# Moving token tiles and weight tiles by 64 bytes within SBUF

## The chip, the cores and the metric

The kernel runs on one NeuronCore of a Trainium2 chip. Its time is the device time of one execution in microseconds. Before the change three timed runs lie between 2381.85 and 2384.83 us, with a median of 2383.91 us.

## The reference, cut to what matters

The reference is a two-layer trunk over 1024 latent tokens of width 1024 with 256 context tokens, all in float32. Nearly all of its arithmetic is in products of a token matrix with a weight matrix:

```python
proj = h @ w_in                                   # both mixers, in
out  = concat([fourier_mix(f_in), y]) @ w_out     # layer 0, out
out  = concat([sgu, pool_out]) @ w_out            # layer 1, out
jnp.square(jax.nn.relu(h @ w1)) @ w2              # each layer's MLP, 1024 -> 4096 -> 1024
```

Around these stand norms with adaLN modulation, a bidirectional SSD scan and a Fourier mix in layer 0, and a chunked spatial gate and a multi-scale pooling in layer 1.

## The kernel before, in words

**How a product is made.** Each float32 operand is split into two tiles of type fp32r, `hi` and `lo`: ScalarE casts `hi` (L489), VectorE subtracts to get `lo` (L490). `mm3` then issues three matmuls for every 128-deep slice, high by high, high by low, low by high. In each matmul one operand is stationary (a 128x128 slice that LDWEIGHTS loads into TensorE) and the other streams through as the moving operand, mostly 512 columns of 4 bytes, a row of 2,048 bytes in each partition. All of this is issued at one line, L478, so the tile names tell the matmuls apart: the profile writes `psg<-hhi,whi` for output, moving tile, stationary tile.

**Two arrangements.** In most products the weights stand still and tokens stream (`psg<-hhi,whi`, `psg<-rlo,whi`, `psg<-h,wlo` and so on): the input projections, both output projections and both MLPs. `Weights.get` and `gemm_tile` hand `mm3` the weight slices first. In two places it is the other way round, because the result is wanted with tokens on partitions: `gate` in `ssd_forward` (`psg<-whi,h`), and `v_gemm` and `v_seq` in `layer1_mixer` (`psg<-whi,hhi`). There a 128-token slice stands still and weights stream. `v_seq(0, 1)` is one such pass of 96 matmuls. After it the pooling group goes on with tokens streaming.

**Where tiles lie.** SBUF pools form two stacks. Pools opened without a side grow upward from the low addresses: `consts` first, from 8,320 to 11,140, then the token pools `h0`, `h1`, `hc` and later `actA`, `actB`, `actC`, the first at 11,168. Pools opened with `side="right"` grow downward from 229,344: among them `w`, the pool of 14 weight tiles of 4,096 bytes, which takes 172,000 to 229,344. Every token tile and every weight tile is a multiple of 512 bytes long, and so are the slices that matmuls take of them, apart from the last blocks of the kernel, which take 1,024-byte halves of token rows. So in the kernel before every moving token row starts at 416 modulo 512 (11,168 = 21 x 512 + 416) and every slice of a weight tile at 480 modulo 512 (172,000 = 335 x 512 + 480). In the two arrangements the same tiles change roles: a streaming weight row starts at 480, a standing token slice at 416. One exception streams tokens against a small projection tile, `wdt`, that lies elsewhere. Pools start at multiples of 32 bytes.

**What sets the order.** TensorE takes its matmuls in program order, with the MLPs interleaving seven products per step (`ORDER`, after a Strassen-like scheme, `PRODUCTS`). Weights come in on the SP queue, scratch stores go out on the POOL queue. VectorE and ScalarE make splits and sums ahead of TensorE.

**The lines that matter below.** `setup` opens the `consts` pool and allocates its first tiles; `run` opens `w`. L478 is `mm`, L489 and L490 are `split`. `startup` is the beginning of the program. The MLP's `FfnNorm` (L198 to L236) stands between each output projection and its MLP.

Of the kernel before, what the change touches and what calls it, by code (L numbers as in the profile page):

```python
# [9 lines left out]
F32 = mybir.dt.float32  # L10
# [6 lines left out]
P = 128  # L17
# [437 lines left out]
class Trunk:  # L455
# [78 lines left out]
    def setup(self):  # L534
        nc, a = self.nc, self.a
        self.cp = self.pool("consts")
        self.dp = self.pool("dram", space=DRAM)
        cp = self.cp
        cmat = cp.tile([P, 2 * P], F32, name="cmat")
        for n, m in ((0, 0), (1, 5)):  # L540
            nc.sync.dma_start(cmat[:, n * P:(n + 1) * P], a["cmat"][:, m * P:(m + 1) * P])
        self.ident, self.ones = cmat[:, :P], cmat[:, P:]
        self.eps = cp.tile([P, 1], F32, name="eps")
        nc.vector.memset(self.eps, EPS)
        self.nhalf = cp.tile([P, 1], F32, name="nhalf")
        nc.vector.memset(self.nhalf, -0.5)
        self.onecol = self.ones[:, 0:1]
        warm = cp.tile([P, 1], F32, name="warm")
        nc.scalar.activation(warm, self.eps, AF.Silu)
        self.cols = cp.tile([P, 2, P], F32, name="cols")  # L550
        self.silu = cp.tile([P, KT, 2], F32, name="silu")
        self.ada = cp.tile([P, 12, KT], F32, name="ada")
        self.adac = cp.tile([P, 2, KT], F32, name="adac")
        self.amul = cp.tile([P, 5, KT], F32, name="amul")
# [1389 lines left out]
```

## Time and profile before

| | before |
|---|---|
| timed runs, median (lowest to highest) | 2383.91 us (2381.85 to 2384.83) |
| the profiled execution's own time | 2386.13 us |
| its span, first to last instruction | 2384.3 us |
| TensorE matmul (PE) busy | 2333.1 us, 98% |
| weight load (PEld) busy | 1837.4 us, 77% |
| VectorE (DVE) busy | 1598.7 us, 67% |
| ScalarE (ACT) busy | 986.6 us, 41% |
| GpSimd (POOL) busy | 178.2 us, 7% |
| mean granted TensorE clock | 0.997 |

Busy shares say how much of the span an engine had an instruction in flight. Matmuls are pipelined: one that is listed with 399 ns overlaps the one behind it, so what a matmul costs is not its listed duration but the distance from its start to the next one's start. That distance is read from the timeline, or from a window with no idle time by dividing its length by the matmuls that start in it.

### The profile page before, as it was taken

To read this page: it belongs to the slowest core of one execution; us is meant where nothing else is said; L and a number is where in the kernel's file an instruction comes from. 1 tells how busy PE (TensorE), PEld (TensorE's weight loads), DVE (VectorE), ACT (ScalarE), POOL (GpSimd) and SP (SyncE) were. 2 spreads that over 40 slices of the span, in tenths; PEclk is the share of its full clock that TensorE was granted. 3 is DMA by queue.
4 is the path that set the end of the run, shared out by engine and by line. 5 is a ranking of instruction groups with operands and counts; after the bars stand their busy time and mean duration, and the time that the engine had idled before them with its cause. 6 is when DMAs were issued, how large, how long until landed. Compare 5 with 4: busy or idle time off the path is not lost. (4 is left out here: it accounts for less than half of the span.)

```text
span 2384.3 us, 27844 instructions
## 1 busy us (share of the span) xinstructions
PE 2333.1 (98%) x10445; PEld 1837.4 (77%) x10445; DVE 1598.7 (67%) x2100; ACT 986.6 (41%) x1385; POOL 178.2 (7%) x301
## 2 busy tenths in 40 slices
PE   7999999999999999999999999999989999999998
PEld 2787777777867888878888887888768888788887
DVE  4777777766378576777877638642496555887785
ACT  3656754443145443623443322121255444543241
POOL 0003002111001010100001000000000101000000
PEclk9999999999999999999999999999999999999999
DMA  8535567658415565873444125652133436754423
GB/s 301 169 125 166 160 217 244 197 183 289 129 58 185 181 219 193 282 250 98 174 171 133 58 71 181 220 208 89 62 117 132 168 126 227 256 186 168 135 82 111
DMA packets 305170, 400.52 MB, mean 168 GB/s; under 512 B 22064, under 2 KB 222380, under 8 KB 297612
## 3 DMA queue, kind: packets, MB, share of 16 engines
q1 hardware_dynamic: 257952, 297.75, 38.4%
q0 software_dynamic: 30656, 91.78, 10.6%
q10 hardware_dynamic: 16427, 9.22, 1.3%
q8 instruction: 82, 1.34, 0.2%
q14 instruction: 53, 0.43, 0.1%
HBM read 282.27 MB, written 116.39 MB: 167 GB/s over the span
## 5 line engine op out<-in xcount | busy, mean ns | idle before, releaser
L478 PE MATMUL psg<-hhi,whi 128*128 128x512 f32 x1088 | 433.4, 399 | 10.0 <-ACT hhi L489 5.7
L478 PE MATMUL psg<-hlo,whi 128*128 128x512 f32 x1088 | 432.2, 397 | 3.9 <-DVE hlo L490 3.9
L478 PE MATMUL psg<-hhi,wlo 128*128 128x512 f32 x1088 | 429.9, 396 | 0.0
L478 PE MATMUL psg<-rhi,whi 128*128 128x512 f32 (+1 forms) x920 | 361.4, 393 | 3.6 <-DVE lat L1545 3.6
L478 PE MATMUL psg<-rlo,whi 128*128 128x512 f32 (+1 forms) x920 | 360.5, 392 | 0.0
L478 PE MATMUL psg<-rhi,wlo 128*128 128x512 f32 (+1 forms) x920 | 360.2, 392 | 0.0
L478 PEld LDWEIGHTS psg<-hhi,whi 128*128 128x128 f32 x1088 | 204.6, 188 | 63.9 <-ACT hhi L489 8.0
L489 ACT CAST whi<-ww 128x1024 fp32r<-128x1024 f32 (+1 forms) x128 | 131.1, 1024 | 284.6 <-DVE wlo L490 233.3
L478 PEld LDWEIGHTS psg<-hlo,whi 128*128 128x128 f32 x1088 | 204.5, 188 | 55.9 <-DVE hlo L490 6.2
L478 PEld LDWEIGHTS psg<-hhi,wlo 128*128 128x128 f32 x1088 | 204.5, 188 | 50.2 <-issue 1.0
L490 DVE TENSOR_TENSOR wlo<-ww,whi 128x1024 fp32r<-128x1024 f32 (+1 forms) x128 | 152.0, 1187 | 106.6 <-PE psg L478 96.7
L1545 DVE SCALAR_TENSOR_TENSOR lat<-psg,ada,lat 128x512 f32<-128x512 f32 (+1 forms) x220 | 163.0, 742 | 81.6 <-PE psg L478 66.9
L478 PEld LDWEIGHTS psg<-rhi,whi 128*128 128x128 f32 x920 | 173.0, 188 | 45.5 <-issue 4.0
L478 PEld LDWEIGHTS psg<-rlo,whi 128*128 128x128 f32 x920 | 173.0, 188 | 40.3 <-issue 0.2
L478 PEld LDWEIGHTS psg<-rhi,wlo 128*128 128x128 f32 x920 | 173.0, 188 | 40.3
L478 PE MATMUL psg<-h,whi 128*128 128x512 f32 (+1 forms) x672 | 197.3, 375 | 4.3 <-DVE h L509 2.8
L489 ACT CAST whi<-ws 128x1024 fp32r<-128x1024 f32 (+1 forms) x96 | 97.8, 1021 | 182.1 <-PE psg L478 98.2
L478 PE MATMUL psg<-yhi,whi 128*128 128x512 f32 x384 | 154.1, 402 | 2.9 <-ACT nss L133 1.8
L478 PE MATMUL psg<-ylo,whi 128*128 128x512 f32 x384 | 152.4, 397 | 0.0
L478 PE MATMUL psg<-yhi,wlo 128*128 128x512 f32 x384 | 152.4, 397 | 0.0
L490 DVE TENSOR_TENSOR wlo<-ws,whi 128x1024 fp32r<-128x1024 f32 (+1 forms) x96 | 113.9, 1187 | 55.3 <-PE psg L478 49.4
L489 ACT CAST rhi<-rlo 128x1024 fp32r<-128x1024 f32 x116 | 115.9, 1047 | 75.6 <-PE psg L478 47.5
(296 smaller groups left out, 3578.4 us busy)
## 6 DMA issues: line engine op xcount, KB each, us to landing
rlo<-r_d SPq DMA_DIRECT2D x58, 1024.0 KB, 6.8
ww<-in_ffn_w_dram SPq DMA_DIRECT2D x190, 256.0 KB, 5.4
r_d<-rt POOLq DMA_DIRECT2D x64, 512.0 KB, 6.5
araw<-in_ada_w_dram SPq DMA_DIRECT2D x56, 512.0 KB, 4.8
r_d<-uc POOLq DMA_DIRECT2D x36, 512.0 KB, 2.9
lat<-lat_d SPq DMA_DIRECT2D x32, 512.0 KB, 10.6
ws<-in_ffn_w_dram SPq DMA_DIRECT2D x62, 256.0 KB, 3.4
wraw<-in_ev_w_in_dram SPq DMA_DIRECT2D x24, 512.0 KB, 7.5
```

Of the source, the lines that this page charges most:

```text
L478: self.nc.tensor.matmul(out, lhsT=lhsT, rhs=rhs, start=start, stop=stop, skip_group_check=onto)
L489: self.nc.scalar.copy(hi, x)
L490: self.nc.vector.tensor_tensor(lo, x, hi.bitcast(F32), ALU.subtract)
L1545: nc.vector.scalar_tensor_tensor(lt, ps, g(ct), lt, ALU.mult, ALU.add)
```

## The change: what it does

Two tiles of 16 float32 per partition (64 bytes) are allocated in `setup` and set to zero on GpSimd. Nothing reads them. One is the first tile of `consts`, so every pool of the low stack starts 64 bytes higher. The other is in a pool of its own that is opened first on the right, so every pool there starts 64 bytes lower. Token rows then start at 480 modulo 512 and weight slices at 416 modulo 512. The constants, the small tiles and all scratch tiles of both stacks move by the same 64 bytes. PSUM and the order of all other instructions stay.

```diff
@@ -536,6 +536,9 @@
         self.cp = self.pool("consts")
         self.dp = self.pool("dram", space=DRAM)
         cp = self.cp
+        self.place = [cp.tile([P, 16], F32, name="place"), self.pool("place", side="right").tile([P, 16], F32, name="wplace")]
+        for t in self.place:
+            nc.gpsimd.memset(t, 0.0)
         cmat = cp.tile([P, 2 * P], F32, name="cmat")
         for n, m in ((0, 0), (1, 5)):
             nc.sync.dma_start(cmat[:, n * P:(n + 1) * P], a["cmat"][:, m * P:(m + 1) * P])
```

## Rows read from the trace of the kernel before

**Rows 1.** The page: busy time, and the granted TensorE clock in forty slices.

```profile
PE 2333.1 (98%) x10445; PEld 1837.4 (77%) x10445; DVE 1598.7 (67%) x2100; ACT 986.6 (41%) x1385; POOL 178.2 (7%) x301
PEclk9999999999999999999999999999999999999999
```

**Rows 2.** Groups by line and form, PE: shape, count | busy us, mean ns | idle.

```profile
L478 PE MATMUL psg<-hhi,whi 128*128 128x512 f32 x1088 | 433.4, 399 | 10.0 <-ACT hhi L489 5.7 <-DVE uc L1585 2.2 <-ACT uc L1583 2.1
L478 PE MATMUL psg<-rhi,whi 128*128 128x512 f32 x888 | 352.0, 396 | 3.6 <-DVE lat L1545 3.6
L478 PE MATMUL psg<-h,whi 128*128 128x512 f32 x512 | 169.2, 405 | 4.3 <-DVE h L509 2.8 <-ACT h L508 1.0 <-ACT xr L118 0.4
L478 PE MATMUL psg<-yhi,whi 128*128 128x512 f32 x384 | 154.1, 402 | 2.9 <-ACT nss L133 1.8 <-ACT yhi L489 1.1
L478 PE MATMUL psg<-h,wlo 128*128 128x512 f32 x256 | 101.9, 399 | 0.0
L478 PE MATMUL psg<-whi,h 128*128 128x512 f32 x256 | 88.5, 417 | 0.0
L478 PE MATMUL psg<-whi,hhi 128*128 128x512 f32 x128 | 51.3, 401 | 0.0
L478 PE MATMUL psg<-h,whi 128*128 128x256 f32 x160 | 28.3, 279 | 0.0
```

**Rows 3.** Timeline, PE, weights streaming (`v_seq`): start us, us, engine, line, instruction.

```profile
1398.19 0.39 PE L478 MATMUL psg<-whi,hhi 128*128 128x512 f32 x1
...
1398.88 0.39 PE L478 MATMUL psg<-whi,hhi 128*128 128x512 f32 x1
...
1418.79 0.39 PE L478 MATMUL psg<-whi,hhi 128*128 128x512 f32 x1
```

**Rows 4.** Timeline, PE, tokens streaming, right behind that pass.

```profile
1420.18 0.39 PE L478 MATMUL psg<-hhi,whi 128*128 128x512 f32 x1
...
1441.18 0.39 PE L478 MATMUL psg<-hhi,whi 128*128 128x512 f32 x1
```

**Rows 5.** Windows of line L478 on PE: length, PE busy (matmuls in flight), clock, DMA.

```profile
1030.00:1318.00 288.00, 288.00 (x1236) 1.00 0.45 153
1780.00:2030.00 250.00, 250.00 (x1073) 1.00 0.51 174
2070.00:2350.00 280.00, 280.00 (x1202) 1.00 0.40 134
```

**Rows 6.** Timeline, PE, 256 columns of context tokens streaming, two stretches.

```profile
109.92 0.39 PE L478 MATMUL psg<-h,whi 128*128 128x256 f32 x2
...
114.68 0.39 PE L478 MATMUL psg<-h,whi 128*128 128x256 f32 x2
...
162.13 0.40 PE L478 MATMUL psg<-h,whi 128*128 128x256 f32 x2
...
164.25 0.40 PE L478 MATMUL psg<-h,whi 128*128 128x256 f32 x2
```

**Rows 7.** Groups by line and form, ACT and DVE, same operation on both sides.

```profile
L489 ACT CAST whi<-ww 128x1024 fp32r<-128x1024 f32 x120 | 126.1, 1051 | 269.5 <-DVE wlo L490 219.6 <-PE psg L478 39.7 <-DMA ww<-in_ffn_w_dram 10.1
L489 ACT CAST rhi<-rlo 128x1024 fp32r<-128x1024 f32 x116 | 115.9, 1047 | 75.6 <-PE psg L478 47.5 <-DMA rlo<-r_d 28.1
L490 DVE TENSOR_TENSOR wlo<-ww,whi 128x1024 fp32r<-128x1024 f32 x120 | 146.4, 1220 | 99.8 <-PE psg L478 89.9 <-ACT whi L489 9.5
L490 DVE TENSOR_TENSOR rlo<-rlo,rhi 128x1024 fp32r<-128x1024 f32 x116 | 138.9, 1218 | 6.6 <-ACT rhi L489 6.0
```

**Rows 8.** Windows, all engines: length, PE, PEld, DVE, ACT, POOL busy, clock, DMA.

```profile
0.00:110.00 110.00, 95.39 (x381) 53.80 (x382) 59.71 (x125) 49.76 (x99) 3.28 (x7) 1.00 0.74 244
688.00:730.00 42.00, 36.17 (x140) 26.40 (x139) 40.14 (x54) 21.41 (x26) 2.61 (x2) 0.92 0.19 61
1732.00:1773.00 41.00, 33.01 (x131) 23.69 (x131) 40.07 (x54) 20.56 (x26) 2.53 (x2) 1.00 0.14 43
2036.00:2063.00 27.00, 25.23 (x108) 19.68 (x107) 19.22 (x20) 16.26 (x18) 3.74 (x7) 1.00 0.93 327
```

**Rows 9.** Timeline, POOL, start of the program.

```profile
0.33 0.10 POOL L1932 MEMSET const-uint8-127<- 128x1 uint8 x1
```

**Rows 10.** Waits of PE: who waited for whom, us in total, times, longest.

```profile
PE psg L478 <- ACT hhi L489: 5.7, 4, 2.3
PE psm L486 <- DMA crow<-in_c_ctx_dram: 5.5, 1, 5.5
```

## The prediction

> **What bounds the kernel now.** [...] So 51 us at most are lost to PE standing idle, and the list of its waits shows them scattered: the two largest sources are 5.7 and 5.5 us [rows 10]. The bound is therefore the rate at which PE takes matmuls, and the next question is what one matmul costs. The listed 396 to 405 ns [rows 2] are latencies that overlap, so I went to the timeline for the distance from start to start.
>
> With weights streaming, one triple of matmuls starts at 1398.19 and the next at 1398.88 us; thirty triples later it is 1418.79 [rows 3]. That is 20.60 us for 90 matmuls, 228.9 ns each. Right behind it, with tokens streaming, 21.00 us pass between 1420.18 and 1441.18 [rows 4], again thirty triples: 233.3 ns each. The two stretches lie in one stage, have the same columns, the same clock and no waits.
>
> The difference is not an accident of this place. The windows of the MLPs are pure token streaming: 280.00 us with 1202 matmuls in flight, of which about two were already running at the left edge, so 1200 starts and 233.3 ns; the other two give 288.00/1234 = 233.4 and 250.00/1071 = 233.4 [rows 5]. Going through the timeline stretch by stretch, leaving out the first matmuls behind a break, I find 58 undisturbed stretches of token streaming, all at 233.3 ([rows 4] is one, the windows of [rows 5] hold the longest), and 20 of weight streaming in the gate and in `v_seq`/`v_gemm`, at 228.8 to 229.8 ([rows 3] is the last of them). No stretch of one kind has the rate of the other.
>
> What differs between the kinds? Streaming rows start at 416 modulo 512 and standing slices at 480 in the first kind; in the second it is 480 and 416. The change makes the first kind's addresses those of the second, and the reverse. Which of the two operands, or their distance, carries the 4.4 ns need not be known: the exchange swaps all three together. This is the step on which everything rests, and it is an inference from two kinds of products that differ in more than the address (which operand is the weight, and which half of SBUF it lies in).
>
> **The change part by part.**
>
> Token streaming, 512 columns. From the groups [rows 2]: 1088 with `hhi,whi` and as many each with `hlo,whi` and `hhi,wlo`, 3264; 888 three times for the `r` tiles, 2664; 512 `h,whi`; 384 three times for the `y` tiles, 1152; 256 `h,wlo`. Together 7848. Each goes from 233.3 to 228.9: 7848 x 4.4 = 34.5 us less.
>
> Weight streaming, 512 columns. 256 `whi,h`, and 128 each of `whi,hhi` and three like it, 768 [rows 2]. Each goes the other way: 768 x 4.4 = 3.4 us more.
>
> Token streaming, 256 columns. 160 `h,whi` [rows 2] and some 190 in smaller groups. These run at two rates with the same addresses: 14 triples from 109.92 to 114.68 us, 113.3 ns each, and six from 162.13 to 164.25, 117.8 each [rows 6]. So here the rate is set by something that the start of a stretch decides. All of them at one rate or the other is worth at most 350 x 4.4/2 = 0.8 us either way; I take zero.
>
> Small true-float32 matmuls, transposes, and columns by one: before, no row compares the same form at both offsets. As bounds I take the same 4.4 ns for each of the remaining 1,480 matmuls or so (10445 less 7848, 768 and 350) either way: 6.5 us, and choose zero, since a stretch of them mixes many offsets already.
>
> VectorE, ScalarE and transfers. The same cast of 1024 columns takes 1051 ns on weight tiles at 480 and 1047 on token tiles at 416; the same subtraction 1220 and 1218 [rows 7]. So the exchange is worth nothing there: 4 ns over the 116 to 120 instructions of a group is 0.5 us, on engines with a third or more of the span free. Transfers into both kinds of tiles keep their length, and move by whole 64 bytes; PE's largest wait for one is 5.5 us at the very start [rows 10], which no SBUF place of a later tile touches. Cost zero.
>
> The two memsets. The nearest row is a memset of 0.10 us on POOL in its first microsecond [rows 9]; POOL has 3.28 us of work in the first 110 us [rows 8]. Both sides: 0 to 0.2 us, hidden by PE's wait for the first transfer of 5.5 us. I take zero.
>
> What of the gain does not arrive. A faster PE gains only where the next thing it needs is there. In 688 to 730 and 1732 to 1773 us VectorE is busy for 40.14 of 42 and 40.07 of 41 us [rows 8] with the split that stands between output projection and MLP; PE's 271 matmuls there gain nothing: 1.2 us. In the first 110 us PE stands for 15 us behind loads and splits [rows 8], with some 190 token matmuls between: 0.8 us. Before each MLP's down half the first set goes out to DRAM and back (2036 to 2063, DMA at 0.93 [rows 8], and the like in layer 0): 108 matmuls each, 1.0 us together. VectorE is next to be late in each, and it is not sped up. Sum 3.0 us; at most I would see 8.
>
> Sum: 34.5 - 3.4 - 3.0 = 28.1 us less. The profiled execution took 2386.1 us, 1.8 more than its span, and would come to 2358; it stands 2.2 us above the median of the runs, 2383.9, so the forecast for the median is 2356.
>
> **The rivals.**
>
> No change, 2384. The 4.4 ns could belong to the arrangement (weights as the moving operand), to the half of SBUF from which PE streams, or to how a stretch starts, as with the 256 columns [rows 6], where two rates 4.5 ns apart occur at the same addresses. For it: those very rows. Against it: with 512 columns 78 stretches, each behind another break, never took the other kind's rate; and a matmul does not know which operand is called a weight. The token pools that stream cover addresses from 11,168 to 125,856 at one rate, so the place within a half does not matter. The change not doing what it says belongs here too: pools start at multiples of 32 bytes, so 64 are kept, which leaves it little.
>
> [...]
>
> Slower, 2415. Suppose streaming from the right half is worth more than the 4.4 ns, and the 480/416 arrangement costs some of it back, hidden in the 228.9. Then the change gives token streaming the cost without the bonus. If it is as large as the difference that I see, 4.4 ns, then (7848 - 768) x 4.4 = 31 us are added: 2415. It decides as soon as the hidden cost is above zero. For it: two unknowns and one difference. Against it: nothing in the rows shows a second term, and the rate is one and the same over three token pools and many weight tiles.
>
> Part of it, 2364 to 2379. Streams fall into a third rate between the two, or the rates mix, as with 256 columns: half of 31 us is 2368. Or VectorE eats more than 8 us.
>
> **How the numbers follow.** Forecast 0.80, part of it 0.04, no change 0.10, slower 0.06. The likeliest one's own range is 2351 to 2364: no loss to other engines and the 256-column gain below, 8 us lost above. To reach 8 in 10 with a little of the partial case I give 2350 to 2370. About 0.2% (4.8 us) is what a measurement can tell from no change; all of the forecast and of the partial case lie beyond it: faster 0.84, same 0.10, slower 0.06.
>
> **What would show it.** Right: windows of the MLP with 1202 matmuls in flight per 280 us now show 1225; triples in `v_seq` 0.70 us apart instead of 0.687; cast and subtraction durations as before; the two windows with VectorE busy throughout as long as before. Wrong: MLP windows still at 233.3, or weight streaming still at 228.9 (then the arrangement or the half carries it), or idle time of PE well above 51 us (then the gain was handed to VectorE or to transfers).

## The result and the profile after

The kernel after takes 2356.78 us (median of four runs, 2354.4 to 2359.49) against 2384.37 us before (four runs). The ratio is 0.9882 with a 95% interval of 0.9863 to 0.9901: 1.2% or 28 us faster. The forecast was 2356 us.

The profiled execution of after took 2354.4 us, the lowest of its four, and its span is 32.0 us shorter than the span of the profile before. Its page, busy time and granted clock, answers to [rows 1]:

```profile
PE 2304.6 (98%) x10445; PEld 1840.7 (78%) x10445; DVE 1596.3 (68%) x2100; ACT 985.7 (42%) x1385; POOL 178.6 (8%) x303
PEclk9999999999999999999999999999999999999999
```

PE has lost 28.5 us of busy time, and is idle for 47.7 us (2352.3 - 2304.6) where it was 51.2 (2384.3 - 2333.1). So 28.5 of the 32.0 us lie inside PE's stream of matmuls, and 3.5 in waits. The timeline of PE in the same two places as [rows 3] and [rows 4], first the streaming weights of `v_seq`, then the streaming tokens right behind (start us, us, engine, line, instruction):

```profile
1382.32 0.40 PE L478 MATMUL psg<-whi,hhi 128*128 128x512 f32 x1
...
1403.32 0.40 PE L478 MATMUL psg<-whi,hhi 128*128 128x512 f32 x1
1404.71 0.40 PE L478 MATMUL psg<-hhi,whi 128*128 128x512 f32 x1
...
1425.32 0.39 PE L478 MATMUL psg<-hhi,whi 128*128 128x512 f32 x1
```

Each pair is thirty triples apart: 21.00 us for 90 matmuls is 233.3 ns, 20.61 us is 229.0. The two kinds have changed rates: weights were at 228.9 and tokens at 233.3. The long windows of the MLPs say the same (length, busy and matmuls in flight of PE, PEld, DVE, ACT, POOL, clock, DMA share, GB/s):

```profile
1012.00:1300.00 288.00, 288.00 (x1260) 236.26 (x1260) 228.34 (x250) 106.80 (x115) 7.20 (x14) 1.00 0.47 161
1752.00:2002.00 250.00, 250.00 (x1094) 205.12 (x1093) 147.96 (x142) 127.66 (x150) 26.18 (x49) 1.00 0.51 175
2037.00:2317.00 280.00, 280.00 (x1225) 229.74 (x1224) 221.13 (x248) 102.92 (x116) 0.00 (x0) 1.00 0.42 142
```

The last has 1225 matmuls in flight in 280 us where [rows 5] has 1202; 250 us hold 1094 for 1073.

The other engines did not change. The same casts and subtractions as in [rows 7] (mean ns behind the busy time):

```profile
L489 ACT CAST whi<-ww 128x1024 fp32r<-128x1024 f32 x120 | 126.1, 1050 | 267.3 <-DVE wlo L490 216.6 <-PE psg L478 39.3 <-DMA ww<-in_ffn_w_dram 11.5
L489 ACT CAST rhi<-rlo 128x1024 fp32r<-128x1024 f32 x116 | 115.9, 1048 | 72.0 <-PE psg L478 47.8 <-DMA rlo<-r_d 24.1
L490 DVE TENSOR_TENSOR wlo<-ww,whi 128x1024 fp32r<-128x1024 f32 x120 | 146.5, 1221 | 93.6 <-PE psg L478 84.1 <-ACT whi L489 9.1
L490 DVE TENSOR_TENSOR rlo<-rlo,rhi 128x1024 fp32r<-128x1024 f32 x116 | 138.8, 1217 | 6.4 <-ACT rhi L489 5.6
```

None differs by more than 1 ns. The two memsets on POOL's timeline, beside [rows 9]:

```profile
0.72 0.11 POOL L541 MEMSET place<- 128x16 f32 x1 [0.29 <-POOLq L1935]
0.77 0.12 POOL L541 MEMSET wplace<- 128x16 f32 x1
```

They end 0.9 us into the span; PE starts behind a transfer of 6.8 us (5.5 before [rows 10]). That the memsets delay this transfer is not likely: E2, E3, E4 and E6 below have one or both of them too, and PE starts there at 4.8 to 5.2 us. The windows of the start and of the two norms, as in [rows 8]:

```profile
0.00:110.00 110.00, 95.57 (x394) 56.64 (x395) 61.01 (x126) 51.07 (x101) 3.45 (x9) 0.98 0.72 245
683.00:725.00 42.00, 35.71 (x137) 26.06 (x136) 40.85 (x54) 21.60 (x27) 2.61 (x2) 0.92 0.18 58
1711.00:1752.00 41.00, 34.81 (x132) 25.35 (x131) 40.08 (x53) 20.60 (x26) 2.54 (x2) 0.92 0.13 43
```

VectorE fills its two windows as before (40.85 of 42 us, 40.08 of 41), and each is as long as before. That shows when the same two matmuls of PE's order are found in both timelines, for the first window in before and in after, then for the second:

```profile
687.71 0.40 PE L478 MATMUL psg<-hlo,whi 128*128 128x512 f32 x1
729.85 0.39 PE L478 MATMUL psg<-hlo,whi 128*128 128x512 f32 x1
...
682.00 0.39 PE L478 MATMUL psg<-hlo,whi 128*128 128x512 f32 x1
724.08 0.39 PE L478 MATMUL psg<-hlo,whi 128*128 128x512 f32 x1
...
1732.15 0.39 PE L478 MATMUL psg<-hhi,whi 128*128 128x512 f32 x1
1772.92 0.39 PE L478 MATMUL psg<-hlo,whi 128*128 128x512 f32 x1
...
1710.96 0.40 PE L478 MATMUL psg<-hhi,whi 128*128 128x512 f32 x1
1751.68 0.39 PE L478 MATMUL psg<-hlo,whi 128*128 128x512 f32 x1
```

The first pair is 42.14 us apart before and 42.08 after, the second 40.77 and 40.72: 256 token matmuls lie in them, and PE's faster rate gained 0.1 us there.

### The profile page after: what moved, and what is told of

It reads as the page before. It is cut to its first block, busy times and chain, and to the rows that moved or that the text cites. A ratio compares the mean times of both kernels' runs of the same rounds, so it can differ in the third digit from the quotient of the medians.

```text
span 2352.3 us, 27846 instructions
## 1 busy us (share of the span) xinstructions
PE 2304.6 (98%) x10445; PEld 1840.7 (78%) x10445; DVE 1596.3 (68%) x2100; ACT 985.7 (42%) x1385; POOL 178.6 (8%) x303
## 3 DMA queue, kind: packets, MB, share of 16 engines
q0 software_dynamic: 30656, 91.78, 10.7%
## 5 line engine op out<-in xcount | busy, mean ns | idle before, releaser
L478 PE MATMUL psg<-hhi,whi 128*128 128x512 f32 x1088 | 431.7, 397 | 9.6 <-ACT hhi L489 5.4
L478 PE MATMUL psg<-hlo,whi 128*128 128x512 f32 x1088 | 430.2, 395 | 2.9 <-DVE hlo L490 2.9
L478 PE MATMUL psg<-hhi,wlo 128*128 128x512 f32 x1088 | 426.0, 392 | 0.0
L478 PE MATMUL psg<-rhi,whi 128*128 128x512 f32 (+1 forms) x920 | 357.4, 389 | 3.7 <-DVE lat L1548 3.7
L478 PE MATMUL psg<-rhi,wlo 128*128 128x512 f32 (+1 forms) x920 | 357.9, 389 | 0.0
L478 PE MATMUL psg<-rlo,whi 128*128 128x512 f32 (+1 forms) x920 | 355.7, 387 | 0.0
L478 PEld LDWEIGHTS psg<-hhi,whi 128*128 128x128 f32 x1088 | 205.7, 189 | 59.4 <-ACT hhi L489 7.7
L478 PEld LDWEIGHTS psg<-hlo,whi 128*128 128x128 f32 x1088 | 205.2, 189 | 48.8 <-DVE hlo L490 5.5
L478 PEld LDWEIGHTS psg<-hhi,wlo 128*128 128x128 f32 x1088 | 205.3, 189 | 46.5 <-issue 1.0
L478 PEld LDWEIGHTS psg<-rhi,whi 128*128 128x128 f32 x920 | 172.8, 188 | 40.3 <-issue 4.2
L478 PEld LDWEIGHTS psg<-rlo,whi 128*128 128x128 f32 x920 | 172.7, 188 | 38.1 <-issue 0.2
L478 PEld LDWEIGHTS psg<-rhi,wlo 128*128 128x128 f32 x920 | 172.8, 188 | 36.3
L478 PE MATMUL psg<-h,whi 128*128 128x512 f32 (+1 forms) x672 | 196.3, 374 | 3.4 <-DVE h L509 2.3
L478 PE MATMUL psg<-yhi,whi 128*128 128x512 f32 x384 | 153.4, 400 | 1.1 <-DVE lat L1467 0.9
L478 PE MATMUL psg<-yhi,wlo 128*128 128x512 f32 x384 | 151.4, 395 | 0.0
L478 PE MATMUL psg<-ylo,whi 128*128 128x512 f32 x384 | 149.5, 390 | 0.0
```

Of the source, the lines that this page charges most:

```text
L478: self.nc.tensor.matmul(out, lhsT=lhsT, rhs=rhs, start=start, stop=stop, skip_group_check=onto)
```

## The experiments

The result shows that the rate goes with the place and not with the arrangement. It doesn't tell which place: the moving row's start, the standing slice's start, or the distance between the two (moving start minus standing start), for the exchange changes all three. Three kernels of the trunk and a map by itself take them apart.

**E1, a map of places.** No trunk: one fp32r pair streams against another, and only the start offsets vary.

```python
for m in range(16):                  # moving row at 32*m bytes modulo 512
    for s in range(16):              # standing slice at 32*s
        # two true-float32 matmuls, then ten triples of 512 columns:
        for i, (w, r) in enumerate(((wh, rh), (wh, rl), (wl, rh))):
            nc.tensor.matmul(ps, lhsT=w[:, st], rhs=r[:, mv], ...)
```

> Leaves out the whole trunk: it only streams one fp32r tile against another, 256 stretches of ten triples (high by high, high by low, low by high; 512 columns), each stretch with its own pair of start offsets in steps of 32 bytes modulo 512, two true-float32 matmuls between stretches. Both operands are neither tokens nor weights and lie side by side in low SBUF. Theory (the places modulo 512 set the rate): moving 416 with standing 480 gives 233.3 ns per matmul, moving 480 with standing 416 gives 228.9; if the moving row's place alone decides, the table varies with the moving offset only; if the standing slice's, with the standing offset only; if their distance, pairs with the same distance share a rate (distance -64: 233.3, +64: 228.9). Rival (the arrangement or the half of SBUF decides): one rate for all 256 pairs. Second rival (how a stretch starts decides): rates scattered over the table without order.

Rates, each from the last 18 of a stretch's 30 matmuls, put together by distance (moving minus standing, modulo 256):

```
distance      0     32     64     96    128          160    192    224   bytes
ns a matmul  226.7  233.3  228.9  233.3  232.4-233.3  234.3  233.3  233.3
```

Each number stands for 32 pairs, and within a column they lie within 0.3 ns (0.9 at 128). No row and no column of the 16 by 16 table has a rate of its own, only the diagonals do, and they repeat after 256 bytes, not 512. Four stretches on the timeline, with moving and standing at 416 and 480 (the kernel before), 480 and 416 (after), 416 and 416, and 160 and 0; each pair of rows is 15 matmuls apart:

```profile
1661.50 0.40 PE L50 MATMUL acc<-rh,wh 128*128 128x512 f32 x1
1665.00 0.39 PE L50 MATMUL acc<-rh,wh 128*128 128x512 f32 x1
...
1883.92 0.39 PE L50 MATMUL acc<-rh,wh 128*128 128x512 f32 x1
1887.35 0.39 PE L50 MATMUL acc<-rh,wh 128*128 128x512 f32 x1
...
1646.73 0.39 PE L50 MATMUL acc<-rh,wh 128*128 128x512 f32 x1
1650.13 0.39 PE L50 MATMUL acc<-rh,wh 128*128 128x512 f32 x1
...
602.23 0.40 PE L50 MATMUL acc<-rh,wh 128*128 128x512 f32 x1
605.75 0.40 PE L50 MATMUL acc<-rh,wh 128*128 128x512 f32 x1
```

3.50, 3.43, 3.40 and 3.52 us over 15. Both rates of the trunk come back in low SBUF with nothing else running, so neither the half of SBUF nor another engine nor a transfer makes them. The map also shows a rate that the trunk did not have: equal places, 226.7.

**E2 and E3, one stack alone.**

```diff
-        self.place = [cp.tile([P, 16], F32, name="place"), self.pool("place", side="right").tile([P, 16], F32, name="wplace")]
+        self.place = [cp.tile([P, 16], F32, name="place")]                                      # E2
+        self.place = [self.pool("place", side="right").tile([P, 16], F32, name="wplace")]       # E3
```

> Only the low stack moves by 64 bytes: token rows and weight slices both at 480 modulo 512. Moving place alone decides: both arrangements at 228.9, time 2384 - 34.5 + 3 = 2352. Standing place alone: both at 233.3, 2384 + 3.4 = 2387. Distance: both arrangements at one common rate, which rows of before do not show, and the same as when only the right stack moves. Rival (arrangement or half): 233.3 and 228.9 as before, 2384.

> Only the right stack moves by 64 bytes: token rows and weight slices both at 416 modulo 512. Moving place alone decides: both arrangements at 233.3, time 2387. Standing place alone: both at 228.9, 2352. Distance: the same rates and time as when only the low stack moves. Rival (arrangement or half): as before, 2384.

E2 took 2337.67 us and E3 2338.59 us (four runs each) against 2384.48 us before: ratios 0.9809 (0.9794 to 0.9823) and 0.9810 (0.9793 to 0.9826). Moving place alone and standing place alone each needed one of the two near 2387 and the other near 2352; both are out. Equal distance, equal time: that is what the distance called for. The same MLP window in E2, then E3:

```profile
2024.00:2304.00 280.00, 279.52 (x1233) 231.21 (x1232) 223.50 (x250) 103.15 (x115) 0.00 (x0) 1.00 0.43 147
```

```profile
2022.00:2302.00 280.00, 279.30 (x1233) 231.15 (x1232) 223.66 (x250) 103.59 (x116) 0.00 (x0) 1.00 0.42 146
```

1233 in flight is 227.5 ns each. Most stretches hold 226.7, some 227 to 228.5, and for the first time such a window has idle time of PE, 0.48 and 0.70 us. So not all of the map's gain arrives. By its rates it would be 7848 x 6.6 + 768 x 2.2 = 53.5 us; the distances from start to start of these two kinds give 45.5 us in E2's timeline and 46.5 in E3's. Some 3.5 us of the rest lie in the first dozen matmuls behind each break, which still run 2 to 3.5 ns slower before the stream settles on 226.7, and 4 to 5 in matmuls next to a wait.

**E4, both stacks the same way.** Low stack 64 bytes up, right stack 448 down, so both places change and their distance does not.

```diff
-        ... self.pool("place", side="right").tile([P, 16], F32, name="wplace")]
+        ... self.pool("place", side="right").tile([P, 112], F32, name="wplace")]
```

> Low stack 64 bytes up, right stack 448 bytes down: token rows at 480, weight slices at 32 modulo 512, so both have moved by +64 and their distance is that of before. Distance decides: 233.3 and 228.9 as before, 2384. Moving place alone decides: token streaming at 228.9, time between 2350 and 2357 (weight streaming from 32 is not known). Standing place alone: the token rate is not known, weight streaming at 233.3.

2385.53 us (ten runs), ratio 1.0003 (0.9992 to 1.0013): no change, though every tile moved. Its MLP window:

```profile
2073.00:2353.00 280.00, 280.00 (x1201) 226.13 (x1200) 215.61 (x241) 101.71 (x114) 0.00 (x0) 1.00 0.39 134
```

**E5, a finer map.** The same stretches with the standing slice 0 to 252 bytes below the moving row in steps of 4 (A), with a place of its own for the standing tile of each triple's third matmul (B), and with 256 columns (C).

```python
for d in range(64): stretch(512, (64, 64), (64 - d, 64 - d))                              # A
for a in range(8):
    for b in range(8): stretch(512, (64, 64), (64 - 8 * a, 64 - 8 * b))                   # B
for d in range(8):
    for _ in range(6): stretch(256, (64, 64), (64 - 8 * d, 64 - 8 * d))                   # C
```

> Leaves out the whole trunk, as the first map did. Part A: 512 columns, moving row fixed, standing slices 0 to 252 bytes below it in steps of 4 bytes (64 stretches of ten triples). Distance theory: 226.7 ns at 0, 228.9 at 64, 233.3 at 32 and 96, 232.7 at 128, 234.3 at 160, 233.3 at 192 and 224. If what meets is a line of 32 or 64 bytes, the rate keeps its value between those points or steps at a few of them; if single 4-byte words meet, it varies at every step. Part B: the standing tile of the first two matmuls of a triple and that of the third at distances of their own (0 to 224 in steps of 32). If a moving row meets the load of the NEXT standing slice, the second matmul of a triple lasts as long as the third's tile says and the third as long as the first's; if it meets its own standing slice, the other way round. Part C: 256 columns, eight distances, six starts each: a rate per distance if the place decides there too; 113.3 and 117.8 by turns at one distance if the start decides.

A: the eight points of the first map come back (226.7, 233.2, 228.9, 233.3, 232.7, 234.3, 233.3, 233.3). Between them the rate changes at most steps: 226.7 at 4 bytes, 233.3 at 8, 243.3 at 100, 226.7 again at 124 and 136. So the rate does not keep one value over 32 or 64 bytes. No distance is faster than equal places.

B: neither of the two forms holds. With 0 for the first tile and 32 for the second the three matmuls of a triple last 233.6, 230.4 and 232.0 ns on average, not 226.7 and 233.3 in some order. Where both tiles have one distance, the map's rates come back; the 56 unequal pairs lie between 228.9 and 235.6, 17 of them at 233.3. Whether a moving row meets the load of the next slice or something of its own stays open.

C: 120.0, 116.4 to 116.9, 117.8, 120.0, 118.8 to 120.0, 117.2, 113.3 and 118.2 to 118.4 ns at 0, 32, ... 224 bytes. Six starts at one distance agree to 0.5 ns (1.2 at 128), so with nothing else running the place decides there too: 113.3 at the distance of before (192), 117.8 at that of after (64). In the whole kernel that is only part of it. E2 and E3 run all such stretches at 119 to 120.3, near the map's value for equal places. But before has both rates at one distance [rows 6], and so has after: of the 13 longer stretches in its timeline ten run at about 117.8 and three at 113.3. What decides between the two there stays open.

**E6, a distance that was not yet tried.**

```diff
-        self.place = [cp.tile([P, 16], F32, name="place"), self.pool("place", side="right").tile([P, 16], F32, name="wplace")]
+        self.place = [cp.tile([P, 56], F32, name="place")]
```

> Only the low stack moves, by 224 bytes: token rows at 128, weight slices at 480 modulo 512, so moving minus standing is 160 modulo 256 for token streaming and 96 for weight streaming, distances that no kernel so far had. Distance theory with the map's rates: token streaming 234.3 ns (233.3 before), weight streaming 233.3 (228.9): 7848 x 1.0 + 768 x 4.4 = 11 us more, 2395. Rival (any unequal move helps, or moving place decides): not slower than before, 2384 or less.

2397.62 us (four runs) against 2386.88: ratio 1.0045 (1.0028 to 1.0062), 10.7 us slower where 11 were expected. Undisturbed token streaming runs at 234.3 and weight streaming at 233.3 ns. The MLP window:

```profile
2080.00:2360.00 280.00, 280.00 (x1197) 225.10 (x1196) 215.63 (x241) 100.87 (x113) 0.00 (x0) 1.00 0.39 134
```

1197 in flight for 1202 before. So the map forecast this whole kernel. In the other direction, E2 and E3, it has the sign right and some 7 us too much.

## Why the prediction was right, point by point

I summed the distances from start to start over the whole timeline of after and of before, matmul by matmul, by kind:

| term | forecast, us | between the two profiles, us |
|---|---|---|
| tokens streaming, 512 columns | -34.5 | -33.9 |
| weights streaming, 512 columns | +3.4 | +2.1 |
| 256 columns | 0 (0.8 either way) | +0.4 |
| all other matmuls | 0 (6.5 either way) | -2.0 |
| start of the first matmul | 0 | +1.3 |
| gain that does not arrive | +3.0 | inside the rows above: 1.0 in the two norm windows |
| sum | -28.1 | -32.1 |

**The step on which all rested**, that the place and not the arrangement carries the 4.4 ns, held. All undisturbed token stretches but one went from 233.3 to 228.9, and all weight stretches from 228.9 to 233.3. E1 shows the same with tiles that are neither tokens nor weights. That any of the three (moving, standing, distance) would do for the forecast was true; it is the distance, and its period is 256 bytes, not 512.

**The weights' term** was 1.3 too high: 2.9 us came in undisturbed matmuls, and matmuls next to a wait gave 0.8 back.

**The term for what other engines keep** is confirmed in one part alone. In the two windows in which VectorE is busy throughout, 256 matmuls gained 0.1 us where 4.4 ns each would have been 1.1: of the 1.2 us put down for them nearly all stayed away, as forecast. The 0.8 us of the first 110 us and the 1.0 us before the MLPs' down halves do not show. From PE's first matmul to the one at 109.92 us before (108.43 after) the gain is 2.8 us, and between 2036 and 2063 us it is 0.40 us for 106 matmuls, nearly the 0.47 of the full rate. Idle time of PE fell by 3.5 us, where the sign of being wrong was a rise.

The clock cost nothing that shows. It is granted at 0.92 in 1711 to 1752 us of after and at 1.00 in 1732 to 1773 of before [rows 8], and the same matmuls take 40.72 and 40.77 us. (The forty 9s of [rows 1] mean 90% or more; the mean before was 0.997, after 0.994.)

**How close the number came is luck in part.** Between the two profiles the gain is 32.1 us, 4 more than the sum. But after's profile is its fastest run, and before's lies 1.8 us above the median of before's runs. By medians the gain is 27.6 us, 3.5 less than 34.5 - 3.4. Whether 3 us were lost or the runs differ by chance can't be told: runs of one kernel scatter by 5 us and more, and medians of before taken beside the experiments lie at 2384.5 and 2386.9. The size is shown to some 4 us, and that the forecast came within 1 us of the median is chance. Its range, too, is wider than its own terms: no loss and 0.8 us at 256 columns give 2352, 8 us lost give 2361, where it says 2351 and 2364.

**The rivals.** No change is out, and slower too: weights as the moving operand have no bonus of their own (E1, and 233.3 in after). Did the arrangement or the half of SBUF decide, E1 would have one rate for all 256 pairs. With nothing else running and a mean clock of 0.999 it has rates from 226.7 to 234.3 ns; what makes the difference inside TensorE is not shown. What spoke for the start of a stretch has one case left among the streams of 512 columns: one token stretch of after runs at the old rate.

```profile
1453.87 0.40 PE L478 MATMUL psg<-hhi,whi 128*128 128x512 f32 x1
...
1458.07 0.40 PE L478 MATMUL psg<-hhi,whi 128*128 128x512 f32 x1
```

Six triples in 4.20 us, 233.3 ns. In E2 and E3 the same stretch starts near 233 ns too and comes down to 226.7 after about eight matmuls. So how a stream starts can hold it at another rate, but in after it did so for about twenty matmuls in 7848.

**The better version.** The exchange took 28 of 46 us that there were. One of the two tiles alone gives 2338 us, 46 us below before, and 0.9809 (up to 0.9823) lies clear of 0.9863, the lower end for the exchange. It costs 64 bytes of each partition. What the forecast lacked was the third pair of places: no row of before had moving and standing at equal places, so no row could price it.

## What to carry to other kernels

Where PE never waits and matmuls still lie further apart than they might, compare the distance from start to start between kinds of products before looking at other engines: two rates at one clock are a lead (here 228.9 and 233.3 ns [rows 3, 4]). In a stream of fp32r matmuls of 512 columns that each load a new slice, look at where the moving rows and the standing slices start modulo 256, and move one stack by a small tile so that they are equal (226.7 ns in E1, where unequal places had up to 234.3). Then look at the 256-column products too: in the map of E5 their best distance is another one (113.3 ns at 192 bytes, 120.0 at 0).

## What was not expected of the hardware

- The rate of fp32r matmuls of 512 columns that each load a new slice depends on moving start minus standing start modulo 256 bytes: 226.7 ns at 0, 228.9 at 64, 234.3 at 160, 233.3 at most others in steps of 32 bytes; in steps of 4 bytes up to 243.3. This is E1 and E5, with nothing else running, and E2, E3, E4 and E6 show it in the whole kernel.
- With 256 columns the order in the map is another: 113.3 ns at 192 bytes, 120.0 at 0. In the whole kernel streams at 64 and at 192 bytes take either 113.3 or 117.8.
- When the standing tiles of a triple lie at two distances, its matmuls don't take the rates of these distances in turn: at 0 and 32 bytes they last 233.6, 230.4 and 232.0 ns, where 226.7 and 233.3 would be the two.
